# An instance norm whose middle units are moved as 64 rows of 64 KB on alternate partitions instead of 128 rows of 32 KB

## The chip, the cores and the metric

The kernel runs on one core of one Trainium2 chip. The metric is the device time of one execution in microseconds (us). The kernel before takes 626.89 us, the median of three runs that lie between 626.77 and 626.9.

## The reference

The input `x` is 4 x 8 x 16 x 256 x 256 float32, so 512 channels of 65536 numbers, 134.2 MB. Each channel is normalised by its own mean and variance and multiplied by one factor of its own:

```python
mu = x.mean(axis=(3, 4), keepdims=True)
var = ((x - mu) ** 2).mean(axis=(3, 4), keepdims=True)
out = (x - mu) / np.sqrt(var + 1e-5) * gamma[None, :, :, None, None]
```

Every byte must be read once and written once. There is little arithmetic.

## The kernel before

The kernel before cuts the input into 32 units of 16 channels. A unit is 4 MB: each of the 128 partitions holds one eighth of a channel, which is 8192 numbers, 32 KB, contiguous in DRAM. Six slots of 4 MB hold units that are being loaded, computed or stored. SyncE (SP) issues the loads and ScalarE (ACT) the stores, so that loads and stores stand in two queues, and the 16 DMA engines serve both.

```python
    S = 8
    K = P // S                      # 16 channels a unit
    F = HW // S                     # 8192 numbers, 32 KB, on each partition
    U = n_ch // K                   # 32 units
    AHEAD = 6
    xv = x.rearrange("b g c h w -> (b g c h w)").rearrange("(u p f) -> u p f", p=P, f=F)
    # ... (ov likewise; pools; constants) ...
    slots = [data.tile([P, F], F32, name=f"xt{i}") for i in range(AHEAD)]

    def load(u, queue):
        queue.dma_start(out=slots[u % AHEAD][:], in_=xv[u])
    # ... (first six loads, gamma, the averaging matrix) ...
    for u in range(U):
        t = slots[u % AHEAD]
        nc.vector.reduce_sum(out=st[:, u, 0:1], in_=t[:], axis=AX.X)
        square = nc.scalar.activation(out=junk[:], in_=t[:], func=ACTF.Square,
                                      accum_out=st[:, u, 1:2])
        # ... (a matmul adds up the 8 partitions of a channel; root, reciprocal, scale) ...
        nc.vector.tensor_scalar(out=t[:], in0=t[:], scalar1=ps[:, 0:1],
                                scalar2=scale[:, u : u + 1], op0=ALU.add, op1=ALU.mult)
        nc.scalar.dma_start(out=ov[u], in_=t[:])
        if u + AHEAD < U:
            load(u + AHEAD, nc.sync)
```

## Time and profile before

| what | value | where it is read |
|---|---|---|
| time; span of the profiled run | 626.89 us; 625.2 us | the times; the head of the page |
| bytes | 134.22 MB each way, 429 GB/s over the span | the page, DMA queues |
| packets that carry the data | 8192 of 32 KB, median 1.213 us, 512 on each of 16 engines | the trace's DMA packets |
| sum of all packet times / 16 | 622.5 us | the same |
| VectorE (DVE), ACT busy | 71%, 38% | the page, busy times |

The first two lines that follow are from the page of the kernel before, its span in 40 slices: the busy share of the DMA engines in tenths and the rate in GB/s. The third is the page's total of packets (it counts 1025 of 4 bytes too, 16 for each of the 64 transfers of x and out and one for gamma).

```profile
DMA  8999999999999999999999999999999999999998
GB/s 369 436 417 424 434 436 436 436 436 437 434 436 434 426 426 430 434 436 436 436 434 434 436 434 434 430 426 430 434 436 436 436 432 434 436 436 434 426 426 365
DMA packets 9220, 268.46 MB, mean 429 GB/s; under 512 B 1025, under 2 KB 1026, under 8 KB 1026
```

The DMA engines are at 9 tenths or more in every slice but the first and the last. The next lines are from the page's costliest groups: line, engine, operation, shapes and count, then busy time in all and the mean ns of one, then the idle time before them and what ended it.

```profile
L103 DVE TENSOR_REDUCE st<-xt 128x1 f32<-128x8192 f32 x32 | 277.9, 8684 | 111.2 <-DMA xt<-in_x_dram 111.2
...
L126 DVE TENSOR_SCALAR xt<-xt,ps,scale 128x8192 f32<-128x8192 f32 x32 | 145.6, 4550 | 1.2
```

The reduction of one unit takes 8.68 us and the normalisation 4.55 us. The reduction waits 111 us in all for loads: the arithmetic has slack, and the loads are what it waits for. SyncE, whose only work is to issue loads, waits in turn for slots to be stored, as this line from the waits of its queue shows (us in total, times, longest):

```profile
SPq L48 <- DMA out_dram<-xt: 536.6, 26, 61.7
```

The windows view gives the busy time of each engine by stretch; the last two columns are the share of the DMA engines and the rate. The share is rough and may come out slightly above 1.

```profile
core 0: us, PE busy (x) PEld busy (x) DVE busy (x) ACT busy (x) POOL busy (x), PEclk, DMA share, GB/s
...
40.00:80.00 40.00, 1.67 (x6) 1.50 (x6) 36.46 (x15) 18.03 (x9) 0.00 (x0) 1.00 1.02 433
120.00:160.00 40.00, 1.12 (x4) 1.01 (x4) 35.21 (x14) 17.66 (x7) 0.00 (x0) 1.00 1.00 432
200.00:300.00 100.00, 2.79 (x10) 2.50 (x10) 72.50 (x26) 39.85 (x17) 0.00 (x0) 1.00 1.01 434
400.00:500.00 100.00, 2.79 (x10) 2.50 (x10) 72.43 (x26) 37.08 (x15) 0.00 (x0) 1.00 1.01 435
```

From start to end nothing but the DMA engines bounds this kernel: 622.5 us of packets in a span of 625.2, so they rest for 2.7 us. The Trainium skill ("DMA: Bandwidth & Descriptors", "Where 436 GB/s comes from") gives a ceiling of 435 GB/s at the 16 ports of the on-chip memory; 32 KB in 1.213 us on 16 engines is 432 GB/s, which agrees. The same place says that about 358 GB/s of DRAM bandwidth is the limit that binds between DRAM and on-chip memory; this kernel, with one core at work, moves 429 GB/s between them over its whole span, so here it does not bind.

Finally the page's DMA issues: count, KB each, and the median us from the issue to the landing of the last byte.

```profile
out_dram<-xt ACTq DMA_DIRECT2D x32, 4096.0 KB, 67.1
xt<-in_x_dram SPq DMA_DIRECT2D x30, 4096.0 KB, 33.8
```

### The profile page before, as it was taken

Reading aid. Unit: us, or ns where it says so; the run is one execution under the profiler, and the core shown is the slowest. Engines: PE = TensorE matmul, PEld = TensorE weight load, DVE = VectorE, ACT = ScalarE, POOL = GpSimd, SP = SyncE. Lnnn points to the kernel's source line nnn. Section 1 sums busy time; section 2 is a strip of 40 time slices with the busy share of each in tenths; the row PEclk is TensorE's granted clock in tenths of the full one; section 3 lists DMA queues with packets and bytes.
Section 4 is the critical chain, followed back from the end, with each engine's and each line's share of the span. In section 5 each row is a group of like instructions: output and inputs, shape, how many; then the busy total and the mean of one; then the engine's idle time right before and its main releaser. Section 6 shows DMA issues by size and latency. Waiting matters only on the chain.

```text
span 625.2 us, 626 instructions
## 1 busy us (share of the span) xinstructions
PE 21.4 (3%) x80; PEld 19.5 (3%) x80; DVE 443.2 (71%) x162; ACT 238.8 (38%) x98; POOL 1.3 (0%) x9
## 2 busy tenths in 40 slices
PE   2000000000000000000000000000000000000000
PEld 2000000000000000000000000000000000000000
DVE  0699999998867668676687766776667867668620
ACT  0444444444444224443244432344423443224400
POOL 0000000000000000000000000000000000000000
DMA  8999999999999999999999999999999999999998
GB/s 369 436 417 424 434 436 436 436 436 437 434 436 434 426 426 430 434 436 436 436 434 434 436 434 434 430 426 430 434 436 436 436 432 434 436 436 434 426 426 365
DMA packets 9220, 268.46 MB, mean 429 GB/s; under 512 B 1025, under 2 KB 1026, under 8 KB 1026
## 3 DMA queue, kind: packets, MB, share of 16 engines
q10 hardware_dynamic: 4898, 142.61, 52.8%
q1 hardware_dynamic: 4320, 125.83, 46.8%
q14 instruction: 2, 0.02, 0.0%
HBM read 134.22 MB, written 134.22 MB: 429 GB/s over the span
## 4 chain that ended last, share of the span: by engine, by line
another core or an unknown queue 64%; DMA 16%; DVE 13%; SPq 1%; PE 1%; issue 0%; ACT 0%
DMA xt<-in_x_dram 9%; DVE st L103 8%; DMA out_dram<-xt 7%; DVE xt L126 4%; SPq L48 1%; PE ps L112 1%; ACT std L117 0%; DVE nvar L113 0%; DVE rstd L121 0%; DVE scale L123 0%
## 5 line engine op out<-in xcount | busy, mean ns | idle before, releaser
L103 DVE TENSOR_REDUCE st<-xt 128x1 f32<-128x8192 f32 x32 | 277.9, 8684 | 111.2 <-DMA xt<-in_x_dram 111.2
L104 ACT ACTIVATE junk<-xt 128x8192 uint8<-128x8192 f32 x32 | 225.0, 7030 | 272.2 <-DMA xt<-in_x_dram 229.0
L126 DVE TENSOR_SCALAR xt<-xt,ps,scale 128x8192 f32<-128x8192 f32 x32 | 145.6, 4550 | 1.2
L117 ACT ACTIVATE std<-nvar,eps_t 128x1 f32<-128x1 f32 x32 | 9.4, 294 | 79.6 <-DVE nvar L113 79.6
L112 PE MATMUL ps<-st,navg 128*128 128x2 f32 x64 | 17.9, 349 | 568.0 <-DVE st L103 568.0
L112 PEld LDWEIGHTS ps<-st,navg 128*128 128x128 f32 x64 | 16.0, 312 | 569.8 <-issue 569.8
L113 DVE TENSOR_SCALAR nvar<-ps 128x1 f32<-128x1 f32 x32 | 9.2, 287 | 23.8 <-PE ps L112 23.8
L121 DVE RECIPROCAL rstd<-std 128x1 f32<-128x1 f32 x32 | 5.3, 164 | 11.6 <-ACT std L117 11.6
L104 ACT ACTIVATION_READ_ACCUMULATOR junk<-xt 128x1 f32 x32 | 6.0, 186 | 0.0
L123 DVE TENSOR_TENSOR scale<-rstd,g_col 128x1 f32<-128x1 f32 x32 | 5.1, 159 | 1.1
L84 PE MATMUL g_ps<-one,g_rep 1*128 1x1 f32 x16 | 3.5, 346 | 2.9 <-DVE g_rep L79 2.9
L84 PEld LDWEIGHTS g_ps<-one,g_rep 1*128 1x128 f32 x16 | 3.5, 325 | 2.9 <-POOL navg L68 2.9
L90 DVE COPY g_col<-g_ps 128x8 f32<-128x8 f32 x1 | 0.2, 166 | 3.7 <-PE g_ps L84 3.7
L74 ACT ACT_TABLE_LOAD x1 | 1.3, 1283 | 2.2 <-issue 2.2
L79 DVE COPY g_rep<-g_row 1x1024 f32<-1x1024 f32 x1 | 0.7, 681 | 2.1 <-DMA g_row<-in_gamma_dram 2.1
L64 POOL TENSOR_SCALAR_AFFINE_SELECT navg<-navg 128x128 f32<-128x128 f32 x1 | 0.4, 403 | 0.1
L68 POOL TENSOR_SCALAR_AFFINE_SELECT navg<-navg 128x128 f32<-128x128 f32 x1 | 0.4, 398 | 0.1
L63 POOL MEMSET navg<- 128x128 f32 x1 | 0.2, 220 | 0.0
L74 ACT ACTIVATE root_eps<-eps_t 128x1 f32<-128x1 f32 x1 | 0.2, 203 | 0.0
L147 POOL MEMSET const-bfloat16-1.0<- 128x1 bf16 x1 | 0.1, 101 | 0.0
L147 POOL MEMSET const-uint8-127<- 128x1 uint8 x1 | 0.1, 101 | 0.0
L147 POOL MEMSET const-float32-0.0<- 128x1 f32 x1 | 0.1, 98 | 0.3 <-issue 0.3
(3 smaller groups left out, 0.3 us busy)
## 6 DMA issues: line engine op xcount, KB each, us to landing
out_dram<-xt ACTq DMA_DIRECT2D x32, 4096.0 KB, 67.1
xt<-in_x_dram SPq DMA_DIRECT2D x30, 4096.0 KB, 33.8
xt<-in_x_dram ACTq DMA_DIRECT2D x2, 4096.0 KB, 33.3
g_row<-in_gamma_dram ACTq DMA_DIRECT2D x1, 0.5 KB
```

What stands on the lines that cost most here:

```text
L48: queue.dma_start(out=slots[u % AHEAD][:], in_=xv[u])
L74: nc.scalar.activation(out=root_eps[:], in_=eps_t[:], func=ACTF.Sqrt)
L79: nc.vector.tensor_copy(out=g_rep[:], in_=g_row[:].rearrange("o (n k) -> o n k", n=NG).unsqueeze(3).to_broadcast([1, NG, K, S]),)
L84: nc.tensor.matmul(out=g_ps[:, n : n + 1], lhsT=g_rep[:, n].rearrange("o k s -> o (k s)"), rhs=one[:], start=True, stop=True,)
L103: nc.vector.reduce_sum(out=st[:, u, 0:1], in_=t[:], axis=AX.X)
L104: square = nc.scalar.activation(out=junk[:], in_=t[:], func=ACTF.Square, accum_out=st[:, u, 1:2],)
L112: nc.tensor.matmul(out=ps[:], lhsT=navg_w, rhs=st[:, u], start=True, stop=True)
L113: nc.vector.tensor_scalar(out=nvar[:, u : u + 1], in0=ps[:, 0:1], scalar1=ps[:, 0:1], scalar2=ps[:, 1:2], op0=ALU.mult, op1=ALU.add,)
L117: nc.scalar.activation(out=std[:, u : u + 1], in_=nvar[:, u : u + 1], func=ACTF.Sqrt, bias=eps_t[:], scale=-1.0,)
L121: nc.vector.reciprocal(out=rstd[:, u : u + 1], in_=std[:, u : u + 1])
L123: nc.vector.tensor_mul(out=scale[:, u : u + 1], in0=rstd[:, u : u + 1], in1=g_col[:, g : g + 1],)
L126: nc.vector.tensor_scalar(out=t[:], in0=t[:], scalar1=ps[:, 0:1], scalar2=scale[:, u : u + 1], op0=ALU.add, op1=ALU.mult,)
```

## The change

The intent is to make fewer and longer packets: a packet has some time that does not grow with its bytes, and 64 KB packets would pay it half as often. So 28 of the 32 units become 14 units of 8 MB with 32 channels, each channel on four partitions, 64 KB contiguous on each. A unit is moved as two transfers, the first half of its rows to the even partitions and the second to the odd ones. At both ends of the kernel 4 MB units of 32 KB rows remain, so that the first arithmetic can start early and the last is short. There are three slots of 8 MB. All first loads are now issued by SyncE.

```diff
-    S = 8
-    K = P // S
-    F = HW // S
-    AHEAD = 6
+    SL = 3
+    FW = HW // 4
+    FN = HW // 8
+    V = n_ch // 32
+    xw = xf.rearrange("(v h r f) -> v h r f", h=2, r=P // 2, f=FW)
+    ow = of.rearrange("(v h r f) -> v h r f", h=2, r=P // 2, f=FW)
+    xn = xf.rearrange("(n p f) -> n p f", p=P, f=FN)
+    on = of.rearrange("(n p f) -> n p f", p=P, f=FN)
     ...
+    slots = [data.tile([P, FW], F32, name=f"xt{i}") for i in range(SL)]
+
+    def load_slot(v):
+        t = slots[v % SL]
+        for h in range(2):
+            if v in (0, V - 1):
+                nc.sync.dma_start(out=t[:, h * FN : (h + 1) * FN], in_=xn[2 * v + h])
+            else:
+                nc.sync.dma_start(out=t[h::2], in_=xw[v, h])
     ... (a second averaging matrix; gamma spread for both kinds of unit;
          the arithmetic of a unit in a function, two squares for a wide unit) ...
+    for v in range(V):
+        t = slots[v % SL]
+        if v in (0, V - 1):
+            for h in range(2):
+                part = t[:, h * FN : (h + 1) * FN]
+                unit(i, part, FN, navg_n, h if v == 0 else 2 + h)
+                nc.scalar.dma_start(out=on[2 * v + h], in_=part)
+                i += 1
+        else:
+            unit(i, t[:], FW, navg_w, NE + v % NW)
+            for h in range(2):
+                nc.scalar.dma_start(out=ow[v, h], in_=t[h::2])
+            i += 1
+        if v + SL < V:
+            load_slot(v + SL)
```

## The prediction

> **What bounds the kernel now.** The DMA engines. The page's row of busy tenths shows DMA at 9 in every slice except the first and last, 429 GB/s over the span; DVE is busy 71% and ACT 38%, and the reduction waits 111 us in all for the load of its tile. The packet records of the trace: 8192 packets of 32 KB at a median 1.213 us, 512 for each of 16 engines, so 621 us of back-to-back packets in a span of 625.2 us. The rest is about 2.7 us without packets, at the start and the end, and about 1.4 us of slower packets (up to 2.3 us) when the first loads start. The Trainium skill ("DMA: Bandwidth & Descriptors", Where 436 GB/s comes from) gives a ceiling of 435 GB/s; 32 KB in 1.213 us on 16 engines is 432 GB/s, within 1% of it. No rearrangement can bring 2%.
>
> **What the change does.** Bytes are the same (134 MB each way). 28 of 32 units become 14 of 8 MB, each moved as two transfers of 64 rows x 64 KB. Packets fall from 8192 of 32 KB to 1024 of 32 KB and 3584 of 64 KB, if a 64 KB row stays one packet. The part of a packet's time that does not grow with bytes can be estimated from this trace: the one 512 B packet took 25 ns and a 32 KB packet 1213 ns, a slope of 27.15 GB/s and about 6 ns fixed. 224 packets fewer per engine at 6 to 8 ns are 1.4 to 1.8 us, all on the critical path, since the engines never rest.
>
> **What it moves.** Per 8 MB unit the reduction becomes about 17.3 us and the normalisation 9.1 us (twice 8.7 and 4.55), with 2 us of small steps: 28.5 us, against 38.7 us of DMA for its load and store. Three 8 MB slots hold the same 24 MB as six of 4 MB; load 38 + compute 28.5 + store 38 us at equal sharing is under the 116 us of a three-slot cycle, so a load or a store is always queued. With all loads on one queue the first unit should land at 12 to 13 us instead of 20.3 and its store be issued near 28 instead of 35.4, but that only reorders transfers. At the end queued stores cover the last units' arithmetic, as before (last store issued at 597.9, end 625.2). Two more matmuls per unit and the set-up on POOL are hidden.
>
> **Partitions.** The Trainium skill ("SBUF — State Buffer", Door 1: The DMA port swizzle) says that rows 0 to 63 reach only half the ports; by its table odd or even rows reach all 16. I expect full rate if the rows are spread one engine to a port, which no run shows yet. This is the main risk.
>
> **Prediction.** 626.9 - 1.6 = 625.3 us; 80% range 622.0 to 629.0. Faster by over 2%: 1%. Within 2%: 94%. Slower by over 2%: 5%.
>
> **What would show it.** 64 KB packets of about 2.42 us; DMA at 9 in every middle slice, mean 430 to 431 GB/s; DVE still waiting for loads; first store near 28 us.
>
> **What would make it wrong.** 64 KB rows cut into 32 KB packets (627); engines colliding on ports (packets clearly over 2.43 us, several per cent slower); three coarse slots leaving both queues empty, seen as DMA slices under 9; a longer tail because the last store waits for arithmetic.

## More of the kernel before

In the trace, the 16 engines finish their shares of one transfer within 0.4 to 1.1 us of each other, and a load lands about 5 us away from the store beside it. The engines keep together; load and store do not.

## The result, and the profile after

| | before | after |
|---|---|---|
| time, median | 626.89 us (626.77 to 627.04) | 733.72 us (733.57 to 741.58) |
| ratio, 95% interval | | 1.173 (1.167 to 1.180) |
| span of the profiled run | 625.2 us | 739.8 us |
| sum of packet times / 16 | 622.5 us | 681.7 us |
| span less that: an engine's mean rest | 2.7 us | 58.1 us |

A ratio here is the mean time of one kernel's fast runs over the mean of the other's in the same rounds, so it is not quite the ratio of the medians that are quoted. All runs in this table are fast ones (a fifth of the change, 735.5 us, is not in its median). The profile is of the longest of the four, 741.58 us, so the two losses in the table add up to a little more than the difference of the medians.

The change costs 107 us. Both kernels move the same bytes, and the records show the packets that the change was meant to make: 3584 of 64 KB and 1024 of 32 KB. The same three lines of the page, of the kernel after:

```profile
DMA  9999999999999999989979979989799899799985
GB/s 390 411 434 425 431 415 436 443 415 365 365 393 354 372 365 337 365 316 337 358 287 372 383 259 379 340 315 369 291 361 361 298 369 354 283 399 390 388 353 239
DMA packets 5637, 268.47 MB, mean 363 GB/s; under 512 B 1025, under 2 KB 1026, under 8 KB 1026
```

Up to slice 9 the rate is that of the kernel before. From slice 10 on, that is from about 165 us, it is mostly between 290 and 400 GB/s and swings. The DMA row is still mostly at 9 and 8, and this is the trap of this profile: an engine that takes longer over the same packet is just as "busy". The windows view of the kernel after says it by stretch:

```profile
core 0: us, PE busy (x) PEld busy (x) DVE busy (x) ACT busy (x) POOL busy (x), PEclk, DMA share, GB/s
...
40.00:80.00 40.00, 1.41 (x6) 1.35 (x6) 29.66 (x6) 14.54 (x5) 0.00 (x0) 1.00 1.00 428
80.00:120.00 40.00, 1.44 (x6) 1.36 (x6) 26.65 (x5) 14.54 (x5) 0.00 (x0) 1.00 1.01 429
120.00:160.00 40.00, 1.41 (x6) 1.36 (x6) 26.65 (x5) 14.54 (x5) 0.00 (x0) 1.00 1.01 437
160.00:200.00 40.00, 1.41 (x6) 1.36 (x6) 26.65 (x5) 14.54 (x5) 0.00 (x0) 1.00 0.99 370
200.00:300.00 100.00, 2.88 (x12) 2.70 (x12) 53.30 (x10) 29.08 (x10) 0.00 (x0) 1.00 0.95 361
300.00:400.00 100.00, 2.88 (x12) 2.71 (x12) 53.30 (x10) 29.08 (x10) 0.00 (x0) 1.00 0.90 338
400.00:500.00 100.00, 2.88 (x12) 2.71 (x12) 53.30 (x10) 29.08 (x10) 0.00 (x0) 1.00 0.90 338
500.00:600.00 100.00, 2.88 (x12) 2.71 (x12) 53.30 (x10) 29.07 (x10) 0.00 (x0) 1.00 0.90 339
600.00:700.00 100.00, 3.44 (x14) 3.21 (x14) 62.72 (x15) 36.49 (x13) 0.00 (x0) 1.00 0.90 363
700.00:740.00 40.00, 0.56 (x2) 0.50 (x2) 18.27 (x6) 7.42 (x3) 0.00 (x0) 1.00 0.70 301
```

Between 120 and 160 us the kernel runs at 437 GB/s, as fast as its predecessor in the same stretch (432; the difference is within the view's roughness, since 64 KB in 2418 ns on 16 engines is 434). In the next 40 us the share of the DMA engines stays at 0.99, and the rate falls to 370. Only later does the share fall too, to 0.90. So there are two losses, and the slower packets come first. The packet records show both:

```
64 KB packets of the kernel after, by start time: mean ns
             loads   stores   busy share of the 16 engines
120-140 us    2446     2418    1.00
140-160 us    2421     2418    1.00
160-180 us    3013     2616    0.99
180-200 us    2961     2623    0.98
300-320 us    2977     2584    0.98
320-340 us    2996     2759    0.78
whole run     2780     2597
```

A 64 KB packet that nothing disturbs takes 2418 ns, twice 1213 ns less 8 ns. That is the gain the change was after, and up to 160 us the kernel has it. Slower packets account for 681.7 - 622.5 = 59 us. The other 55 us (58.1 - 2.7) are engines at rest, and what they rest for can be seen in the landings. Before the slowdown the engines finish their shares of one load within 2 to 5 us of each other. From 260 us on, the last engine is 27 to 33 us behind the first: 10 of the 16 lag, and 6 finish within 3 us of the first. The trace does not name a packet's engine, but 37% of the 64 KB packets between 260 and 600 us, about 6 in 16, take the bare time. A slot is free, and a load complete, only when the slowest engine is done, so the quick engines run out of work. The arithmetic feels this as waits:

```profile
L128 DVE TENSOR_REDUCE st<-xt 128x1 f32<-128x16384 f32 (+1 forms) x18 | 275.8, 15323 | 260.1 <-DMA xt<-in_x_dram 260.1
...
L154 DVE TENSOR_SCALAR xt<-xt,ps,cf 128x16384 f32<-128x16384 f32 (+1 forms) x18 | 141.6, 7869 | 0.7
```

The reduction of an 8 MB unit takes 17.23 us (the group's mean mixes in the eight short ones of the ends), the normalisation 8.83, as predicted. VectorE's wait for loads has grown from 111 to 260 us. SyncE's line and the DMA issues of the long transfers:

```profile
SPq L58 <- DMA out_dram<-xt: 592.4, 24, 58.7
```

```profile
xt<-in_x_dram SPq DMA_DIRECT2D x28, 49.8
out_dram<-xt ACTq DMA_DIRECT2D x28, 46.4
```

Both directions now take nearly 50 us from issue to landing, for 4 MB. Before, a load took half as long as a store. This is the first sign that loads and stores have fallen into step. The issues and landings of single transfers in the trace say so plainly:

```
kernel after, us: issued -> last engine landed
load  120.27 -> 164.14    store 110.11 -> 158.96   5.2 us apart, about one row of each
load  139.74 -> 186.36    store 155.98 -> 183.51   2.9 us apart
load  158.96 -> 209.41    store 156.48 -> 209.59
load  235.09 -> 285.13    store 238.14 -> 285.31
load  285.44 -> 335.35    store 289.02 -> 335.53
load  385.63 -> 435.65    store 389.50 -> 435.83
```

(The landing of the store issued at 110.11 is read from the load that it releases at 158.96.) Until then a load and the store of the same half, thus of the same parity of partitions, land 5 to 8 us apart. Within two transfers they draw together, and from 209 us on their last engines finish 0.2 us apart, pair after pair. Each queue has its next transfer waiting, so both go on together. That the fall in speed begins just there, between 160 and 180 us, is a coincidence in time so far; the experiments had to show whether it is a cause.

### The profile page after: what moved, and what is told of

Read it like the earlier page. It is cut to its first block, busy times and chain, and to the rows that moved or that the text cites. A ratio compares the mean times of both kernels' runs of the same rounds, so it can differ in the third digit from the quotient of the medians.

```text
span 739.8 us, 623 instructions
## 1 busy us (share of the span) xinstructions
PE 25.8 (3%) x108; PEld 24.4 (3%) x108; DVE 430.0 (58%) x99; ACT 234.7 (32%) x84; POOL 5.2 (1%) x19
## 4 chain that ended last, share of the span: by engine, by line
DMA 54%; DVE 22%; another core or an unknown queue 20%; PE 1%; SPq 0%; issue 0%; ACT 0%; ACTq 0%; DVEq 0%
DMA xt<-in_x_dram 30%; DMA out_dram<-xt 24%; DVE st L128 14%; DVE xt L154 7%; PE ps L143 0%; SPq L58 0%; PE ps L145 0%; PE ps L144 0%; ACT cf L151 0%; DVE cf L147 0%; DVE cf L152 0%; DVE cf L153 0%; PE ps L141 0%; SPq L56 0%
## 5 line engine op out<-in xcount | busy, mean ns | idle before, releaser
L128 DVE TENSOR_REDUCE st<-xt 128x1 f32<-128x16384 f32 (+1 forms) x18 | 275.8, 15323 | 260.1 <-DMA xt<-in_x_dram 260.1
L154 DVE TENSOR_SCALAR xt<-xt,ps,cf 128x16384 f32<-128x16384 f32 (+1 forms) x18 | 141.6, 7869 | 0.7
L143 PE MATMUL ps<-st,navg_w 128*128 128x1 f32 x28 | 8.1, 359 | 620.4 <-DVE st L128 620.4
L151 ACT ACTIVATE cf<-cf,eps_t 128x1 f32<-128x1 f32 x18 | 5.3, 294 | 75.9 <-DVE cf L147 75.9
L143 PEld LDWEIGHTS ps<-st,navg_w 128*128 128x128 f32 x28 | 7.0, 311 | 621.5 <-DVE st L128 510.4
L147 DVE TENSOR_SCALAR cf<-ps 128x1 f32<-128x1 f32 x18 | 5.2, 288 | 24.6 <-PE ps L145 21.7
L144 PE MATMUL ps<-st,navg_w 128*128 128x1 f32 x28 | 7.9, 352 | 0.0
L145 PE MATMUL ps<-st,navg_w 128*128 128x1 f32 x28 | 7.9, 352 | 0.0
L144 PEld LDWEIGHTS ps<-st,navg_w 128*128 128x128 f32 x28 | 7.7, 333 | 0.0
L145 PEld LDWEIGHTS ps<-st,navg_w 128*128 128x128 f32 x28 | 7.6, 333 | 0.0
L152 DVE RECIPROCAL cf<-cf 128x1 f32<-128x1 f32 x18 | 3.0, 164 | 6.5 <-ACT cf L151 6.5
L141 PE MATMUL ps<-st,navg_n 128*128 128x2 f32 x8 | 2.2, 349 | 72.8 <-DVE st L128 72.8
L153 DVE TENSOR_TENSOR cf<-cf,g_col 128x1 f32<-128x1 f32 x18 | 2.9, 159 | 0.6
L90 POOL TENSOR_SCALAR_AFFINE_SELECT navg_w<-navg_w 128x128 f32<-128x128 f32 x7 | 3.0, 422 | 0.5
```

The lines of the kernel that those rows point to most:

```text
L90: nc.gpsimd.affine_select(out=navg_w[:], in_=navg_w[:], pattern=[[-8, P // 8], [-1, 8]], compare_op=ALU.not_equal, fill=-1.0 / HW, base=-d ...
L128: nc.vector.reduce_sum(out=st[:, i, 0:1], in_=t, axis=AX.X)
L141: nc.tensor.matmul(out=ps[:], lhsT=w, rhs=st[:, i, 0:2], start=True, stop=True)
L143: nc.tensor.matmul(out=ps[:, 0:1], lhsT=w, rhs=st[:, i, 0:1], start=True, stop=True)
L144: nc.tensor.matmul(out=ps[:, 1:2], lhsT=w, rhs=st[:, i, 1:2], start=True, stop=False)
L145: nc.tensor.matmul(out=ps[:, 1:2], lhsT=w, rhs=st[:, i, 2:3], start=False, stop=True)
```

## The experiments

Five theories stood at the start: the length of the rows by itself; alternate partitions, hence ports; three coarse slots that leave queues empty; and the DRAM addresses of a load and a store, in two forms (their fixed distance of 16 MB, and the range that a transfer covers). The later ones, that load and store in step on the same partitions disturb each other, and that the store's row decides, came from the results. The letters in the quoted expectations are those of the moment; the text after each names the theory in words. Times of the kernel before, run beside each, were 626.8 to 627.3 us. A kernel called "wrong" moves data without computing, so its output is not the reference's; all others gave the correct result. Each of the three was run once, so that the state of the run is unknown; the differences read from them are 9% or more, and stages that were repeated agree (128 rows of 64 KB in step: 98.3, 98.7 and 98.8 us; opposite halves: 79.8 twice).

### e1_pad: the same kernel with rows cut at 32 KB

A gap of 64 bytes in the middle of each partition's row makes two packets of 32 KB out of one of 64 KB, in both directions. Slots, partitions, transfers, DRAM addresses and order stay.

```diff
-    slots = [data.tile([P, FW], F32, name=f"xt{i}") for i in range(SL)]
+    slots = [data.tile([P, 2, FN + 16], F32, name=f"xt{i}") for i in range(SL)]
-                nc.sync.dma_start(out=t[h::2], in_=xw[v, h])
+                nc.sync.dma_start(
+                    out=t[h::2, :, :FN], in_=xw[v, h].rearrange("r (c f) -> r c f", c=2))
```

(The store and the arithmetic follow the same shape.)

> The changed kernel with a gap of 64 bytes in the middle of each partition's row of a slot, so that a 64 KB row is moved as two runs of 32 KB; odd and even partitions, slots, order and units stay. Theory A (packets of 64 KB make the 16 DMA engines lose step, which packets of 32 KB do not): about 627 us, packets of 32 KB at 1.21 us, landings of a transfer within 1 us of each other. Theory B (alternate partitions collide): stays at 725 to 745 us. Theory C (loads and stores 16 MB apart run side by side on colliding addresses): stays at 725 to 745. Theory D (three slots of 8 MB are too coarse): stays there too. If the packets stay 64 KB on the DRAM side, the run says little about A.

Measured: 627.76 us, ratio 1.0014. All 8192 packets of 32 KB are near the bare time (loads 1220 ns, stores 1213 ns in the mean). The page's slices:

```profile
DMA  8999999999999999999999999999999999999997
GB/s 368 433 404 435 435 435 435 435 433 435 431 435 435 429 425 431 430 436 435 435 435 433 435 433 431 431 435 435 430 425 433 431 435 435 435 433 433 435 435 341
```

So alternate partitions, three coarse slots and the DRAM layout cost nothing by themselves. It is not the row alone that has changed, however: in this kernel a load and the store beside it land about 9.7 us apart, not 0.2. So the length of the rows is part of the cause, or the timing that came with it; the stages of m2 tell.

### e2_all_rows: 64 KB rows on all 128 partitions in one transfer

```diff
-    xw = xf.rearrange("(v h r f) -> v h r f", h=2, r=P // 2, f=FW)
+    xw = xf.rearrange("(v p f) -> v p f", p=P, f=FW)
-                nc.sync.dma_start(out=t[h::2], in_=xw[v, h])
+            elif h == 0:
+                nc.sync.dma_start(out=t[:], in_=xw[v])
```

(The averaging matrix and gamma follow: four neighbouring partitions are a channel.)

> Middle units as one transfer of 128 rows x 64 KB on all partitions, three slots of 8 MB. Theory A (64 KB packets): still slow, 700 to 760 us, landings spread over tens of us. Theory B (alternate partitions): back to about 626. Theory C (address distance of 16 MB): still slow. Theory D (coarse slots): still slow, perhaps slower than 734, as a slot is freed only when all 8 MB are stored.

Measured: 631.63 us, ratio 1.0076; the expectation of the row length as the sole cause, 700 to 760 us, missed. Loads of 64 KB take 2436 ns, stores 2422. The engines land within 6 us of each other, and here a load and the store beside it happen to stay about one row (5 us) apart. Long rows alone are not enough. Most of the few microseconds above the kernel before are lost at the end: the last store is issued at 617.3 us, after arithmetic that the store before it, done on 15 of the 16 engines by 616.1, no longer covers.

### e6_col_halves: 8 MB units on all partitions, moved as column halves

```diff
-                nc.sync.dma_start(out=t[h::2], in_=xw[v, h])
+                nc.sync.dma_start(out=t[:, h * FN : (h + 1) * FN], in_=xw[v, :, h * FN : (h + 1) * FN])
```

> Middle units of 8 MB on all 128 partitions, moved as two transfers of 128 rows x 32 KB (the halves of each 64 KB row), three slots. Theory A (64 KB packets): about 627 us. Theory B (alternate partitions): about 627. Theory C (address distance): still slow, over 700. Theory D (coarse slots): still slow, over 700.

Measured: 628.18 us, ratio 1.0021. With 32 KB rows, coarse units and three slots are harmless a second time.

### e4_order: load and store on opposite partitions

The order of the halves alternates from unit to unit, so that a load and the store beside it fall on odd and even partitions, and 12 or 20 MB apart in DRAM.

```diff
-        for h in range(2):                       # loads
+        for h in ((0, 1), (1, 0))[v % 2]:
-            for h in range(2):                   # stores
+            for h in ((1, 0), (0, 1))[v % 2]:
```

> The changed kernel with the two transfers of a unit in the order even, odd for the loads of even units and odd, even for their stores (reversed for odd units), so that a load and a store that run side by side are 12 or 20 MB apart and not 16 MB. Theory C (address distance): back to about 626 us. Theories A, B and D: stays at 725 to 745 us.

Measured: 649.31 us (646.65 and 651.97), ratio 1.036, in neither of the two expected ranges. Loads take 2472 ns, stores 2428: the packets are nearly back to the bare time, with rows of 64 KB on alternate partitions. So something that load and store share when they run beside each other is the cause. Part of the rest is a fault of this kernel: its last unit's halves were loaded in the wrong order, which leaves about 15 us of arithmetic bare at the end. But its engines still lose step: from 300 to 560 us the last one ends a load 18 to 20 us after the first (e14 takes this up). Two things were exchanged at once here, the partitions and the DRAM distance. The next two runs separate them.

### e11_swap_dram and e12_swap_rows: one of the two exchanged alone

e11 exchanges which half in DRAM goes with which parity in every second pair of units; load and store keep the same partitions in the same order, but are 12 or 20 MB apart in DRAM:

```diff
-                nc.sync.dma_start(out=t[h::2], in_=xw[v, h])
+                nc.sync.dma_start(out=t[h::2], in_=xw[v, h ^ swap(v)])
```

e12 leaves the order in DRAM and exchanges the partitions:

```diff
-                nc.sync.dma_start(out=t[h::2], in_=xw[v, h])
+                nc.sync.dma_start(out=t[h ^ swap(v) :: 2], in_=xw[v, h])
```

Here `swap(v)` is `(v // 2) % 2`; stores and gamma follow.

> The changed kernel, but in every second pair of middle units the even partitions take the second half of the unit's DRAM range and the odd partitions the first. Order of transfers by partition, slots, 64 KB rows all stay; only the DRAM distance between a load and the store beside it changes, from 16 MB to 12 or 20. Theory C2 (DRAM addresses exactly 16 MB apart, at the same time, slow both): 626 to 655 us, 64 KB loads at under 2.5 us. Theory E (the same partitions of two slots read and written at the same time): stays at 725 to 745. Theory A2 (any 64 KB packets on 64 alternate rows lose step): stays at 725 to 745.

> The same exchange, but now the order by DRAM address is kept and the order by partition is changed: a load and the store beside it are 16 MB apart in DRAM and on opposite partitions. Theory C2 (DRAM): stays at 720 us or more. Theory E (partitions): 626 to 660 us. Theory A2: stays. A load's first half here waits for the second half of a store, which can add some us by itself and would blur a slow result, not a fast one.

Measured: e11 735.51 us (loads 2785 ns, stores 2561), ratio 1.173, as slow as the change itself; e12 644.77 us (641.24 and 648.29; loads 2462, stores 2443), ratio 1.028, unclear at 2%, but far below e11. The distance in DRAM is innocent, and the partitions are what remains. One doubt stays with e12: the first half of a load into a slot now waits for the second half of a store, which also moves the transfers in time. Its loads and stores land about 5 us apart, and not 0.2 as in the change and in e11, so that partitions and timing changed together (m2 separates them). e11 has no such doubt.

### e8_interleaved: neighbouring rows in DRAM on neighbouring partitions

Row p goes to partition p, moved as the even and the odd rows, so each transfer spans 8 MB of DRAM with gaps instead of 4 MB without.

```diff
-                nc.sync.dma_start(out=t[h::2], in_=xw[v, h])
+                nc.sync.dma_start(out=t[h::2], in_=xw[v, h::2])
```

> The layout of the run with one transfer of 128 rows (partition p holds row p of the 8 MB), but moved as two transfers of even and odd rows: alternate partitions and 64 KB packets stay, the DRAM rows of one transfer are now 128 KB apart, and an engine's DRAM range is another (256 KB apart from its neighbour's, not 128 KB). Theory A2 (64 KB packets on alternate partitions lose step): 700 to 745 us. Theory F (it is the DRAM range of each engine, 128 KB apart, with 64 KB packets): about 632. Theory C2: slow too, as load and store stay 16 MB apart: over 700.

Measured: 736.16 us, ratio 1.174 (loads 2823 ns, stores 2635). The range in DRAM is innocent too. Load and store of the same half land 0.2 us apart here as well.

### e5_halves: partitions 0 to 63 and 64 to 127 instead of even and odd

```diff
-                nc.sync.dma_start(out=t[h::2], in_=xw[v, h])
+                nc.sync.dma_start(out=t[h * 64 : h * 64 + 64], in_=xw[v, h * 64 : h * 64 + 64])
```

> Two transfers of 64 x 64 KB onto partitions 0 to 63 and 64 to 127 instead of even and odd ones. If rows 0 to 63 reach half of the ports (the skill's port page), two engines share a port: 64 KB packets near 4.8 us while only loads run (up to 25 us), and 1100 us or so in all if loads and stores of the same half coincide; if ports carry a read and a write at once, less, 750 to 1000. If the ports do not matter here: the same as the changed kernel, 725 to 745.

Measured: 881.16 us, ratio 1.405.

```profile
DMA  9999999999999999999999999999999999999994
GB/s 394 229 290 257 284 279 257 299 320 317 311 290 308 311 332 299 314 290 347 320 344 317 302 314 332 335 332 320 320 317 341 332 299 320 281 302 341 269 279 202
```

While only loads run, at 20 to 40 us, a 64 KB packet takes 4.9 us, twice the bare time, and slices 2 to 7, in which stores join, move 229 to 290 GB/s. This is what the Trainium skill says ("SBUF — State Buffer", "Door 1: The DMA port swizzle"): partitions 0 to 63 reach only 8 of the 16 ports. The choice of even and odd rows was right for the ports, and the ports do not explain the change's loss: the same kind of load on alternate partitions ran at a median of 2418 ns in the same 20 us.

### m1_phases: the transfers alone, in stages

A kernel that is wrong, without arithmetic. It fills three slots and then, in stages, loads 2 x 8 MB into two slots while it stores 2 x 8 MB from the third; a tiny operation on all slots ends each stage. Only the shape and the order of the transfers differ from stage to stage:

```python
    for form, load_order, store_order, late in [
        ("alt64",  (0, 1), (0, 1), False), ("alt64",  (0, 1), (1, 0), False),
        ("alt64",  (0, 1), (0, 1), True),  ("full64", (0, 1), (0, 1), False),
        ("full32", (0, 1), (0, 1), False), ("alt32",  (0, 1), (0, 1), False),
        ("alt64",  (0, 1), None,   False), ("alt64",  None,   (0, 1), False)]:
```

"alt64" is the change's form, "full" is all 128 partitions, the number is the row in KB, and "late" puts one extra row for each engine at the head of the stores.

> DMA alone, wrong result on purpose: eight stages of 16 MB of loads beside 16 MB of stores, nothing computed, all queues emptied between stages, so that a load and a store start together on each engine. 1: 64 rows x 64 KB, even then odd partitions, loads and stores in the same order. 2: stores odd then even. 3: as 1, but each engine stores one row more first, so that a store is one row behind. 4: 128 rows x 64 KB. 5: 128 rows x 32 KB. 6: as 1 with rows cut to 32 KB. 7: loads of 1 alone. 8: stores of 1 alone. Theory E1 (a 64 KB row read and a 64 KB row written in the same partition at the same time slow each other): 1 and 4 slow (64 KB packets at 2.6 us or more), 2, 3 fast (2.42), 5 and 6 fast (1.213), 7 and 8 fast. Theory E2 (reads and writes on the same set of alternate partitions collide, whichever row): 1 and 3 slow, 2 and 4 fast. Theory G (only the pipeline of the whole kernel, not the pairing, makes engines lose step): all fast.

Measured (length of a stage, mean ns of loads and stores): opposite partitions 79.8 us (2535, 2418); same partitions with the store one row behind 84.4 us including the extra row (2561, 2418); 128 rows of 64 KB in step 98.3 us (3058, 2641); loads alone 39.9 us (2457); stores alone 38.9 us (2422); the two 32 KB stages together 156.8 us, 78.4 each. The means of loads contain the first few packets of a stage, which are slow in every stage. The separator failed for 32 KB columns and, with it, for the first stage, the one that mattered most: it ran together with the filling of the slots, and was repeated in the next kernel. What holds already: either direction alone is at full rate on alternate partitions, 128 rows of 64 KB in step are slow, and in the two 32 KB stages load and store land 0.2 us apart and the packets still take 1213 ns in the median. So alternate partitions are no part of the cause. It suggests that e2 had been quick because its loads and stores stayed a row apart.

### m2_phases: the same with a sound separator, and sizes between

Wrong. Seven stages: (1) even and odd 64 KB rows, same order, in step; (2) 128 rows of 64 KB, store one row behind; (3) the same in step, with the DRAM side of the stores moved by 1.6 MB; (4) rows of 48 KB in step; (5) rows of 56 KB in step; (6) rows of 32 KB in step; (7) even and odd 64 KB rows, stores in the opposite order.

```diff
-            nc.vector.memset(t[:, 0:1], 0.0)
+            nc.vector.memset(t[:, FN - 1 : FN + 9], 0.0)
     ...
+        ("alt64", (0, 1), (0, 1), False, 0),  ("full64", (0,), (0,), True, 0),
+        ("full64", (0,), (0,), False, 409600), (12288, (0,), (0,), False, 0),
+        (14336, (0,), (0,), False, 0),         ("full32", (0, 1), (0, 1), False, 0),
+        ("alt64", (0, 1), (1, 0), False, 0),
```

> DMA alone again, wrong result on purpose, with the barrier between stages mended (in the run before, stages 1 and 6 began before the stage ahead had ended). Seven stages: 1: 64 rows x 64 KB, even then odd, loads and stores in the same order. 2: 128 rows x 64 KB, each engine stores one row more first. 3: 128 rows x 64 KB in step, store addresses in DRAM moved by 1.6 MB. 4: 128 rows x 48 KB in step. 5: 128 rows x 56 KB in step. 6: 128 rows x 32 KB in step. 7: 64 rows x 64 KB, stores odd then even. Theory E1 (long rows of the same partition read and written at the same time slow each other): 1 and 3 slow (mean 64 KB packet 2.6 us or more, stage 90 us or more), 2 and 7 fast (2.42 to 2.5, 80 to 85 us), 6 fast; 4 and 5 tell where between 32 and 64 KB it begins: slow there means over 5% above 1.817 and 2.117 us. If it is the DRAM address after all, 3 is fast. If odd and even rows were innocent in the changed kernel, 1 is fast.

The windows view of this kernel, one row for each stage in this order (start and end, length, then the columns as before):

```profile
core 0: us, DVE busy (x) POOL busy (x), PEclk, DMA share, GB/s
64.60:162.00 97.40, 0.33 (x6) 0.00 (x0) 1.00 0.90 334
164.10:248.80 84.70, 0.33 (x6) 0.00 (x0) 1.00 0.95 396
250.70:349.40 98.70, 0.33 (x6) 0.00 (x0) 1.00 0.88 329
351.40:422.20 70.80, 0.33 (x6) 0.00 (x0) 1.00 0.91 344
424.10:510.10 86.00, 0.33 (x6) 0.00 (x0) 1.00 0.89 331
512.00:591.30 79.30, 0.13 (x2) 0.00 (x0) 1.00 0.97 417
594.20:674.00 79.80, 0.00 (x0) 0.00 (x0) 1.00 0.94 407
```

The rows begin about 1.4 us after a stage's first packets, so the view's rates are up to a few per cent below a stage's bytes over its length, and the latter are used here. All stages but (4) and (5) move 33.6 MB, (2) one row for each engine more.

| stage | us | GB/s | mean ns: loads, stores |
|---|---|---|---|
| 1 alternate 64 KB, in step | 97.4 | 345 | 3045, 2659 |
| 7 alternate 64 KB, opposite | 79.8 | 420 | 2543, 2418 |
| 2 all, 64 KB, one row behind | 84.7 | 409 | 2549, 2509 |
| 3 all, 64 KB, in step, DRAM moved | 98.7 | 340 | 3003, 2673 |
| 4 all, 48 KB, in step | 70.8 | 356 | 2125, 2109 |
| 5 all, 56 KB, in step | 86.0 | 342 | 2683, 2309 |
| 6 all, 32 KB, in step | 79.3 | 423 | 1250, 1217 |

Stages 1 and 7 differ in nothing but the order of the stores' halves, and in 17.6 us. In stage 1 a load and a store of 64 KB together take 5.70 us instead of 4.84, a factor of 1.18, and the stage takes 1.22 times as long as stage 7. That is the size of the change's loss, 1.17 over a run whose first 160 us are undisturbed. Moving the DRAM side does not help. Rows of 32 KB do not suffer, rows of 48 KB do.

### e13_longer_end: e2 with a longer end of 4 MB units

This was an attempt to repair e2's bare end and beat both kernels: the last two 8 MB units become four of 4 MB.

```diff
-            if v in (0, V - 1):
+            if v in (0, V - 2, V - 1):
```

> All partitions, 64 KB rows, one transfer of 8 MB for each middle unit as in the run of 631.6 us, with the last two 8 MB done as four 4 MB units and not one as two. That run lost its time at the end, where the last unit's load landed at 603 us and its arithmetic stood bare; with a finer end: 624.5 to 627 us. If the loss is elsewhere (slower packets in the middle), it stays at 630 or more.

Measured: 634.0 us, ratio 1.0112; the expected 624.5 to 627 missed. Between 540 and 580 us, where 64 KB stores ran beside 32 KB loads, the stores took 2769 and then 2988 ns in the mean (of 20 us each). That was not foreseen, and made the next question: whose row must be long?

### e14_order_end: e4 without its fault at the end

```diff
-        for h in range(2):                       # loads
+        for h in (1, 0) if v % 2 and v < V - 1 else (0, 1):
-            for h in range(2):                   # stores
+            for h in ((1, 0), (0, 1))[v % 2]:
```

> The run with exchanged order of halves (649 us) loaded the two halves of the last unit in the wrong order, so that the half computed first landed last and about 15 us of arithmetic stood bare at the end. The same with the last unit in its proper order. Theory E1 (rows of the same partition read and written at the same time): 630 to 638 us, 64 KB loads at 2.42 to 2.50 us. If exchanging the order does not mend the changed kernel by itself: over 645.

Measured: 642.63, 642.94, 641.09 and 630.8 us. Only the last lies in the expected 630 to 638. The three others count as slow runs, being over 1.5% above the fastest. The profile fell in one of them; its packets are at 2478 and 2427 ns. All four are far from 734. What scatters them is open. The profiled one shows where its time went: from 380 us on the last engine ends most loads 16 to 24 us after the first, the last load lands at 610.9 us, and 15 us of arithmetic stand bare again before the last store (626.0 us). In that run, which counts as slow, the right order at the end was not enough; whether the same holds for e4 is not shown.

### m3_phases: whose row, and how long

Wrong. All 128 partitions, load and store in step; the first number is the load's row in KB, the second the store's: 36/36, 40/40, 44/44, 64/32, 32/64, 64/64.

```python
    for load_form, store_form in [(9216, 9216), (10240, 10240), (11264, 11264),
                                  ("full64", "full32"), ("full32", "full64"), ("full64", "full64")]:
```

> DMA alone, wrong result on purpose, six stages of two loads beside two stores in step on the same partitions (128 rows): 1: rows of 36 KB both ways, 2: 40 KB, 3: 44 KB, 4: loads of 64 KB beside stores of 32 KB, 5: loads of 32 KB beside stores of 64 KB, 6: 64 KB both ways. Theory E1: 6 slow (1.15 to 1.25 of the time of 423 GB/s); 1 to 3 show whether the loss grows with the length of the row or begins at one length; if both rows must be long, 4 and 5 are fast (415 GB/s or more), if one long row is enough, both are slow (under 390 GB/s).

The windows view of this kernel, a row for each stage (the rows begin about 2 us before a stage's first packets):

```profile
core 0: us, DVE busy (x) POOL busy (x), PEclk, DMA share, GB/s
60.70:106.40 45.70, 0.33 (x6) 0.00 (x0) 1.00 0.96 400
108.30:163.90 55.60, 0.33 (x6) 0.00 (x0) 1.00 0.95 376
166.00:228.30 62.30, 0.33 (x6) 0.00 (x0) 1.00 0.97 367
230.30:290.40 60.10, 0.33 (x6) 0.00 (x0) 1.00 0.97 410
292.40:363.90 71.50, 0.33 (x6) 0.00 (x0) 1.00 0.97 352
365.90:464.70 98.80, 0.33 (x6) 0.00 (x0) 1.00 0.93 340
```

| rows: load, store | us | GB/s | mean ns: loads, stores |
|---|---|---|---|
| 36, 36 KB | 45.7 | 413 | 1449, 1384 |
| 40, 40 KB | 55.6 | 377 | 1595, 1726 |
| 44, 44 KB | 62.4 | 370 | 1786, 2033 |
| 64, 32 KB | 60.1 | 419 | 2505, 1213 |
| 32, 64 KB | 71.5 | 352 | 1423, 2912 |
| 64, 64 KB | 98.8 | 340 | 3029, 2694 |

Long loads beside short stores run at full rate; short loads beside long stores do not. The store's row decides, which neither of the two expectations for stages 4 and 5 had foreseen. With equal rows, the loss sets in between 36 and 40 KB. The kernel before, at 32 KB, is below that.

### e15_short_stores: the change with only its stores cut to 32 KB

If the store's row decides, two lines must repair the change, with its loads, slots and partitions left alone:

```diff
-                nc.scalar.dma_start(out=ow[v, h], in_=t[h::2])
+                for c in range(0, FW, FN):
+                    nc.scalar.dma_start(out=ow[v, h][:, c : c + FN], in_=t[h::2, c : c + FN])
```

> The changed kernel, odd and even partitions, same order, 64 KB loads; only the stores of the middle units are cut into rows of 32 KB (each store as two, one for each half of the columns). Theory E3 (it is the store of a row over 36 KB that suffers beside a load of the same partition, the load's length does not matter): 624 to 632 us, all packets at their bare time. If long loads are enough to lose, or if odd and even rows in themselves do: over 690.

Measured: 631.54 us (631.21 to 631.81), ratio 1.0072. That gives back 102 of the 107 us. Loads of 64 KB take 2442 ns, stores of 32 KB 1215.

```profile
DMA  8999999999999999999999999999999999999996
GB/s 366 433 420 441 414 414 456 414 458 431 402 433 439 456 437 398 431 437 429 431 433 435 456 433 418 433 425 435 440 441 437 404 431 435 433 431 433 431 433 296
```

One reservation: the cut also moves the transfers in time. From 130 us on, the loads that land within 1 us of a store do so beside one of the other half, thus on the other partitions, so most of this run cannot tell the length of the store's row from the partitions. Two loads before that do land 0.2 us from a store of the same half (103.8 and 118.4 us): from 88 to 118 us the loads take 2437 ns and the stores 1213. m3 shows the effect of the row over whole stages in step.

### e17_full_short: all partitions, 64 KB loads, 32 KB stores

The best guess for a kernel that beats both: e2 with its stores cut the same way.

> All partitions, one load of 8 MB in 64 KB rows, stores in rows of 32 KB (two of 4 MB). Theory E3: no slow packets at the end either, where the version with 64 KB stores lost (631.6); half of the packets saved, so 625.5 to 628 us, which is within noise of the kernel before or at best 1 us under it.

Measured: 628.48 us (628.04 to 628.97), ratio 1.0026, just outside the expected 625.5 to 628. No version beat the kernel before. With 8 ns saved on each of 224 packets, at most 1.8 us of it was ever to be had, and stores that must stay at 32 KB give up half.

## Why the prediction was wrong

What it had right:

- **The bound.** The DMA engines were and are what bounds the kernel; VectorE and ScalarE had slack in both.
- **The packets.** 3584 of 64 KB and 1024 of 32 KB were recorded, as counted; a 64 KB row stays one packet.
- **The bare price.** A packet's fixed part is 2 x 1213 - 2418 = 8 ns; 6 to 8 had been estimated. The intended gain exists in undisturbed packets, and is about 0.3%.
- **The arithmetic.** 17.23 and 8.83 us for a unit, 17.3 and 9.1 predicted; the first unit landed at 13.0 us, 12 to 13 predicted; the first store was issued at about 28 us, as predicted.
- **The ports.** Even and odd rows reach the full rate in either direction; e5 shows what the other cut costs.

What failed: the step "224 packets fewer per engine at 6 to 8 ns are 1.4 to 1.8 us, all on the critical path, since the engines never rest". The number of packets was right; the term that was mis-sized is the time of one. It was taken from packets that run undisturbed (2.42 us), for all packets, without asking what the same engine does beside it. Measured over the whole run it is 2.78 us for loads and 2.60 for stores, 59 us in all. And "the engines never rest" fell with it: a load or a store was always queued, as predicted, but not on every engine. With 10 engines behind 6, an engine rested 55 us more than before in the mean; that it was mostly the quick ones is read from the landings, not measured.

The prediction also waved away the thing that decides: of the earlier first loads and stores it said that this "only reorders transfers". How they stand to each other in time was harmless only as long as the stores' rows were short. The sign of failure that it listed, packets clearly over 2.43 us, did come, but with a cause that was not the one named. It is not that the rows reach too few ports: stage 7 of m2 uses the same rows at 420 GB/s. DMA slices under 9, its sign of slots that are too coarse, came too, but with a load in flight all the while, and e1 and e6 keep the three slots at full rate.

What the runs show in its place: when a load and a store run in step over the same partitions, though in different slots, and the store's rows are 40 KB or longer, both slow down, for 64 KB by 1.18 in packet time. In the stages each condition was taken away by itself, and the rate came back each time:

| condition taken away | run | result |
|---|---|---|
| same partitions at once | m2 stage 7 against 1 | 79.8 us against 97.4 |
| in step (store one row behind) | m2 stage 2 against m1's 128 rows of 64 KB | 84.7 us, with an extra row, against 98.3 |
| long rows in the store | m3, 64/32 against 64/64 | 419 GB/s against 340 |
| long rows in both | m2 stage 6 against m1's 128 rows of 64 KB | 79.3 us against 98.3 |

The whole kernels agree, but none of the quick ones took away one condition alone. In the three that lose 107 to 109 us (the change, e11, e8) a load and a store of the same half land 0.2 us apart from 210 us on. In e1 (627.76 us) the nearest landings are about 9.7 us apart, in e2, e12 and e14 about 5, and in e15 (631.54 us) most loads run beside a store of the other half. So what they add is that load and store are in step on the same partitions in each of these three, and in no quick one but for the first stretch of e15, whose stores are short. (e5 is slow too, for its ports.)

And these were shown innocent: alternate partitions (e1, m2), three coarse slots (e1, e6), the distance in DRAM (e11, m2 stage 3), the range in DRAM (e8), long rows in loads (m3).

How the whole kernel comes to be in step is argued, not shown by a run of its own: up to 164 us a store and the load beside it land 5 to 8 us apart, then 2.9, then 0.2. What draws them together is not shown. Once they are, each queue has its next transfer behind it, of the same half and as long, so they end together and the next pair starts together.

Left open: the mechanism inside the chip, and why it begins between 36 and 40 KB; why 10 engines are slowed and 6 are not; the scatter of e14; how much of the gain of e12, e4 and e14 is their changed timing. "The same engine reads and writes the same partition at the same moment" is the simplest reading of "in step on the same partitions", but the runs were not made to show single engines against single partitions.

## What to carry to other kernels

Before you lengthen the rows of a transfer, ask what else the DMA engines move at that moment: a packet time measured undisturbed is the price of that packet only as long as no transfer in the other direction walks the same partitions in step. If rows of stores over 36 KB are wanted beside loads, keep the two apart, by other partitions or by a row in time, or leave the stores at 32 KB; a fixed part of 8 ns in 1.2 us was worth no risk. And read the rate (GB/s) and the packet times beside the DMA engines' busy share, because a slowed engine looks as busy as a full one.

## What the Trainium skill lacked or had wrong

- No page that was read says that a store slows a load that is in step with it on the same partitions, and the reverse. "DMA: Bandwidth & Descriptors" is where it belongs: alternate 64 KB rows take 97.4 us in step, 79.8 us when the store's halves come in the opposite order, for the same 33.6 MB (m2, stages 1 and 7).
- "DMA: Bandwidth & Descriptors", "Rules for kernel authors", advises to coalesce many small transfers into a large one; it speaks of the size of a transfer and gives no upper bound for the rows in it. Here, in step, stores with rows of 36 KB keep 413 GB/s and of 40 KB have 377, of 64 KB 340 (m3).
- "SBUF — State Buffer", "Can I just issue two DMAs to hit both halves?", says that only one transfer over all 128 partitions reaches all 16 ports. Transfers of 64 even or odd partitions, one after the other, reach the full rate too: loads alone moved 16.8 MB in 39.9 us, 421 GB/s, and stores alone in 38.9 us, 431 GB/s (m1). For partitions 0 to 63 the page's port map holds: 64 KB packets of 4.9 us instead of 2.42 (e5).
- "DMA: Bandwidth & Descriptors", "Where 436 GB/s comes from", says without a condition that the DRAM side, about 358 GB/s for a core, binds between DRAM and on-chip memory. With one core at work the kernel before moved 429 GB/s over its span, half of it read and half written, and loads alone moved 421 (m1). The page itself, under its measured loads, has 425 GB/s for one core alone and keeps 358 for two at work; the sentence lacks that condition. The page's other ceiling, 435 GB/s, agrees.
- "DMA: Bandwidth & Descriptors" has a fixed cost of a packet in cycles, for small ones; no page that was read gives the time for packets of 32 KB and more: 8 ns here (2 x 1213 - 2418).
